# Block sums of w_out for the seven half-size products: added by DMA instead of by the vector engines

## The chip, the cores and the metric

The program runs on one core of one Trainium2 chip. The metric is the device time of one execution in microseconds (us). Five engines matter: TensorE (PE in the profile, its weight loads PEld), VectorE (DVE), ScalarE (ACT), GpSimd (POOL) and SyncE (SP), which in the kernel before issues every DMA. Each engine takes its instructions strictly in the order in which the program lists them; an instruction that waits holds up everything behind it on its engine.

## The reference, cut to what matters

A decoder layer: one input projection, two attention mixers, two branch projections, a gated merge, one output projection. The change touches only the last line, `merged @ w_out`, with `merged` of 512 x 1024 and `w_out` of 1024 x 1024, float32, and the residual `x` added.

```python
y_a = o_a * jax.nn.silu(z_a)
y_b = o_b * jax.nn.silu(z_b)
g_m = jax.nn.sigmoid(gate_m)
merged = g_m[..., :D_MODEL] * (y_a @ w_branch_a[l]) + g_m[..., D_MODEL:] * (y_b @ w_branch_b[l])
x = x + merged @ w_out[l]
```

## The kernel before, in words

**Arithmetic.** Every float32 product is made of three TensorE products of rounded halves: a tile is cast to a rounded high part (`wh`, `mh`, ...) and the rest is subtracted out as a low part (`wl`, `ml`, ...). So a weight block needs a load, a cast (ACT or POOL) and a subtraction (DVE or POOL) before TensorE can use it; the helper `mm3` (L399) then issues high x high, low x high, high x low.

**The output projection.** `merged` and `w_out` are cut in two by two blocks and multiplied by a scheme of seven half-size products instead of eight (Strassen's, in Winograd's form). A block of `w_out` is 512 x 512 and lies in four tiles of 128 x 512 (256 KB each), called b11, b12, b21, b22. The right factors of the products are: 1: b11; 7: b22 - b12; 5: t1 = b12 - b11; 6: t2 = b22 - t1; 2: b21; 3: b22; 4: b21 - t2. Four of the seven are sums, with four tiles each, so there are sixteen tile sums. A `Sum` object (L273 ff.) stands for one tile: `srcs` are its blocks in HBM, `keep` the number of a buffer `ws` in which t1 and then t2 stay, `prior` the sum that it continues, `home` says that its split halves go to the attention tiles' pool. All blocks are loaded by SP into rotating buffers `wq` (tag `ph`, six of them, shared with attention), then a `tensor_sub` on DVE or POOL makes the sum (L284, L286), then the split follows (L346, L348: cast; L350: low part).

**Order.** TensorE's work is listed by a generator per stream; the other engines' work is put in chains (`Chain`), each with planned costs, and a heap deals the chains' next steps to the engine that would end them first by those planned costs (`either` means DVE or POOL). What results is one fixed list per engine. Products 1 and 7 are made among the last branch projections (`EARLY`), the other five at the end in `output()`: first 5 and 6 interleaved, then 2, 3 and 4. SP's list holds block loads, the weight loads `wr` of gates and branches (`Stream.load`), the loads of the residual `xr`, and the stores.

Of the kernel before, what the change touches and what calls it, by code (L numbers as in the profile page):

```python
# [15 lines left out]
ALU = mybir.AluOpType  # L16
# [5 lines left out]
P = 128  # L22
# [20 lines left out]
LAT = 60  # L43
EARLY = {4:1,5:7}
PACE = 800
SHARE_A = 1.0
SHARE_F = 1.1
SHARE_C = 1.0
# [42 lines left out]
def hybrid_kernel(ctx: ExitStack, tc: tile.TileContext, x, x0, xT, wtok, wchan, gains, w1,  # L91
# [14 lines left out]
    def nm(s):  # L106
        uid[0] += 1
        return f"{s}{uid[0]}"
# [4 lines left out]
    now = [0.0]  # L113
    heap, seq = [], itertools.count()
    free = {"A": 1900.0, "D": 0.0, "P": 800.0, "Q": 400.0}
# [6 lines left out]
    held = {k: [] for k in RES}  # L122
    waiters = {k: [] for k in RES}
    owner, keep = {}, []
# [3 lines left out]
    def ca(n):  # L128
        return 93 + 0.834 * n

    def cap(n):
        return 51 + 0.834 * n

    def cd(n):
        return 65 + 1.045 * n

    def cg(n):
        return 180 + 2.08 * n
# [4 lines left out]
    def either(n):  # L143
        return {"d": cd(n), "P": cg(n)}
# [10 lines left out]
    class Chain:  # L155


        def __init__(c, t=None, held=False):
            c.t = now[0] if t is None else t
            c.q = deque()  # L160
            c.held = held
# [52 lines left out]
    def dma(dst, src, n, t=None):  # L214

        nc.sync.dma_start(out=dst, in_=src)
        free["Q"] = max(free["Q"], (now[0] if t is None else t) + 1000) + max(450, n * P / 360)
        return free["Q"] + 1000
# [6 lines left out]
    def alloc(tag, name, shape=(P, 512), dt=F32):  # L225
        pool, n = RES[tag]
        t = pool.tile(list(shape), dt, name=nm(name), tag=tag, bufs=n)
        keep.append(t)
        h = held[tag]
        if len(h) >= n:  # L230
            h.remove(min((z for z in h if z[0] is not None), key=lambda z: z[0]))
        owner[id(t)] = o = [None, tag]
        h.append(o)
        return t
# [4 lines left out]
    def release(t, when=None):  # L239
        o = owner[id(t)]  # L240
        o[0] = now[0] if when is None else when
        for c in waiters[o[1]]:
            c.t = max(c.t, o[0])
            c.push()
        waiters[o[1]].clear()
# [27 lines left out]
    class Sum:  # L273
# [2 lines left out]

        def __init__(z, srcs, keep=None, put=False, prior=None, home=False):
            z.srcs, z.keep, z.put, z.prior, z.home = srcs, keep, put, prior, home
            z.raw, z.t, z.c, z.left, z.next = [], 0.0, Chain(held=True), 1, None
            if prior:  # L280
                z.left += 1
                prior.next = z
            if len(srcs) == 2:
                z.c.do(either(512), lambda e: e.tensor_sub(z.dst(), z.raw[0], z.raw[1]), lambda: z.raw[1])  # L284
            elif keep is not None:
                z.c.do(either(512), lambda e: e.tensor_sub(z.dst(), z.raw[0], wsum[keep]))  # L286
            if put:
                z.c.call(lambda: release(z.raw[0], z.c.t))

        def dst(z):  # L290
            return wsum[z.keep] if z.put else z.raw[0]

        def fire(z, t):
            z.t = max(z.t, t)
            z.left -= 1
            if not z.left:
                z.c.start(max(now[0], z.t))

        def end(z):
            if not z.put:  # L300
                release(z.raw[0], z.c.t)
            if z.next:
                z.next.fire(z.c.t)

    wsum = []

    class Stream:
# [17 lines left out]
        def load_sums(w):  # L325
            ld = Chain()
            for z in w.tiles:
                if isinstance(z, Sum):
                    for src in z.srcs:
                        def f(z=z, src=src):  # L330
                            t = alloc("ph", "wq")
                            z.raw.append(t)
                            z.t = max(z.t, dma(t, src, 2048))
                        ld.do(None, f, None, "ph")
                    ld.call(lambda z=z: z.fire(z.t))

        def split_sum(w, i):
            z = w.tiles[i]
# [103 lines left out]
    def att(name, dt=F32R):  # L442
        return ap_.tile([P, 512], dt, name=nm(name), tag="a")
# [920 lines left out]
    def merged(c, j, m):  # L1364

        lo_, hi_ = slice(0, 256), slice(256, 512)
        a, b = att("mh"), att("ml")

        def sub(c, dst, x, y):
            c.do(either(256), lambda e: e.tensor_sub(dst, x, y))  # L1370

        def part(c, h, l, src):
            c.do({"A": ca(src.shape[-1])}, lambda e: e.copy(h, src))  # L1373
            c.do(either(src.shape[-1]), lambda e: e.tensor_sub(l, src, h.bitcast(F32)))
        if j < 4:
            q = att("ms", F32)
            sub(c, q[:, lo_], m[:, lo_], m[:, hi_])
            part(c, a[:, lo_], b[:, lo_], m[:, lo_])
            part(c, a[:, hi_], b[:, hi_], q[:, lo_])
            ms.append((m, q, c))  # L1380
            A11.append((a[:, lo_], b[:, lo_], c))
            S3.append((a[:, hi_], b[:, hi_], c))
            return
        i = j - 4
        n, q, prior = ms[i]
        assert not prior.q
        if i % 2 == 0:
            one.append((att("s1h"), att("s1l")))
        o = slice(i % 2 * 256, i % 2 * 256 + 256)
        u, v = (z[:, o] for z in one[-1])  # L1390
        x, y = att("sh"), att("sl")
        d, f = Chain(held=True), Chain(held=True)
        c.do(either(256), lambda e: e.tensor_add(q[:, hi_], n[:, hi_], m[:, hi_]))
        c.call(lambda: d.start(c.t))
        sub(c, n[:, lo_], q[:, hi_], n[:, lo_])
        sub(c, n[:, hi_], m[:, lo_], n[:, lo_])
        c.call(lambda: f.start(c.t))
        part(d, u, v, q[:, hi_])
        part(c, x, y, n)
        part(f, a, b, m)  # L1400
        A12.append((a[:, lo_], b[:, lo_], f))
        A22.append((a[:, hi_], b[:, hi_], f))
        S1.append((u, v, d))
        S2.append((x[:, lo_], y[:, lo_], c))
        S4.append((x[:, hi_], y[:, hi_], c))
# [36 lines left out]
                    if e == 4:  # L1442
                        f(t, (p, Chain(now[0] + 230)), o)

    def add(z, t, r, col, frees=False, o=slice(0, 512)):
        p, c = z
        key = 2 * r + t, col
        dst = xr[key]
        pend[key] = pend.get(key, 0) + 1
        c.do({"D": cd(o.stop - o.start)}, lambda e: e.scalar_tensor_tensor(  # L1450
            dst[:, o], p[:, o], 0.25, dst[:, o], op0=ALU.mult, op1=ALU.add), p if frees else None)
        c.call(lambda: pend.__setitem__(key, pend[key] - 1))

    def send(z, t, r, col, o=slice(0, 512)):
        key = 2 * r + t, col

        def f():
            assert pend[key] == (o.stop < 512 and not z[2:])
            dma(out[key[0] * P:(key[0] + 1) * P, col * 512 + o.start:col * 512 + o.stop], xr[key][:, o],
                4 * (o.stop - o.start))  # L1460
        z[1].call(f)
# [3 lines left out]
    def hold(z, name):  # L1465
        held_[name].append(z[0])
        z[1].mark(("read", id(z[0])))
# [8 lines left out]
    def out7():  # L1476
        def f(t, z, _):
            add(z, t, 1, 0)
            add(z, t, 1, 1)
            p = held_["1"][t]  # L1480
            z[1].do({"A": cap(512)}, lambda e: e.copy(z[0], p)).mark(("read", id(p)))
            hold(z, "7")
        yield from products((S3, "ss", f))
        i = tiles.index(right[5][0])
        for k in range(4):
            Chain(now[0] + PACE * k).call(lambda k=k: W.split_sum(i + k))

    early = {1: out1, 7: out7}

    def output():  # L1490
        def five(t, z, _):
            add(z, t, 1, 1)
            hold(z, "5")

        def six(t, z, _):
            add(z, t, 1, 1)
            send(z, t, 1, 1)
            add(z, t, 0, 1)
            hold(z, "6")
        yield from products((S1, "to", five), (S2, held_["7"], six))  # L1500
        for left, ps, r, col in ((A12, held_["1"], 0, 0), (S4, held_["5"], 0, 1), (A22, held_["6"], 1, 0)):
            def f(t, z, o):
                for q in (slice(0, 256), slice(256, 512)):
                    if o.start <= q.start < o.stop:
                        y = z if o.stop - o.start > 256 else (*z, 1)
                        add(z, t, r, col, q.stop == o.stop, q)
                        send(y, t, r, col, q)
            yield from products((left, ps + ps[1:] * (left is A22), f))
# [21 lines left out]
    now[0] = 3500.0  # L1530
    A, F, C, X = Run(attention(), SHARE_A), Run(gemms(), SHARE_F), Run(cmp(), SHARE_C), Run(x_rms(), 100.0)
    runs = [X, A, F, C]
    while any(r.live for r in runs):
# [9 lines left out]
        r = min(ok, key=lambda q: q.vt)  # L1543
# [80 lines left out]
```

## Time and profile before

| | |
|---|---|
| time, median of 3 runs | 468.33 us (467.44 to 468.35) |
| span of the profiled execution, first to last instruction | 466.7 us; it is the only time that the profile has of that execution, 1.6 us under the median of the timed runs |
| instructions | 7421 |
| TensorE clock granted, mean | 0.996 |
| DMA | 54.34 MB, mean 116 GB/s |

In the profile's rows a group is: line, engine, operation, `out<-in`, shape, count, busy time. In the timeline and the chain of waits the first column is the start and the second the length, both in us. A wait is shown in square brackets with the engine and line that ended it. In the table of stretches each engine has its busy time in us and its count of instructions, then come the granted clock, the mean busy share of the DMA engines and GB/s.

### The profile page before, as it was taken

The page shows a single profiled execution, that of the slowest core. Times are in us where ns is not written, and L with a number is a line of the kernel's source. Part 1 is how long each engine was busy: PE and PEld are TensorE (multiplying, and loading weights), DVE is VectorE, ACT ScalarE, POOL GpSimd, SP SyncE. Part 2 cuts the span into 40 slices and gives each one's busy share as a digit, 9 for nine tenths or more (in the row PEclk, how much of TensorE's full clock was granted, in tenths as well). Part 3 has the DMA queues.
Part 4 walks back from the last instruction along what each step waited for, and adds up shares of the span by engine and source line. Part 5 has one row for each costly group of instructions (what it writes and reads, how often), then busy time and mean ns, then how long its engine had stood idle before and what let it go on. Part 6 is the DMA issues. An engine that isn't in the chain of part 4 may idle for free.

```text
span 466.7 us, 7421 instructions
## 1 busy us (share of the span) xinstructions
PE 460.7 (99%) x2432; PEld 389.4 (83%) x2432; DVE 365.0 (78%) x852; ACT 264.1 (57%) x609; POOL 167.8 (36%) x215
## 2 busy tenths in 40 slices
PE   9989999999999999999999999999999999999997
PEld 8768887899788998888888888888888788887886
DVE  5767589788978868796877777687776887589994
ACT  7652547676677745656766653386765533263530
POOL 0115135644746323123554531455553140015110
PEclk9989999999999999999999999999999999999999
DMA  8752343364413622322223032301311588642162
GB/s 293 231 168 78 102 126 96 80 178 141 145 49 104 190 67 49 98 82 77 49 81 89 20 109 76 107 8 46 93 45 55 194 270 308 203 145 90 30 185 103
DMA packets 30486, 54.34 MB, mean 116 GB/s; under 512 B 3376, under 2 KB 5296, under 8 KB 30448
## 3 DMA queue, kind: packets, MB, share of 16 engines
q1 hardware_dynamic: 30448, 53.87, 38.1%
q8 instruction: 19, 0.31, 0.3%
q14 instruction: 19, 0.16, 0.1%
HBM read 51.11 MB, written 2.75 MB: 115 GB/s over the span
## 4 chain that ended last, share of the span: by engine, by line
PE 95%; DVE 2%; ACT 1%; issue 1%; DMA 1%; POOL 0%; DVEq 0%; ACTq 0%; POOLq 0%
PE pgc L399 31%; PE pgt L399 17%; PE pbr L399 9%; PE po L399 8%; PE O L1034 6%; PE pt L999 6%; PE pgf L609 5%; PE sps L952 3%; PE sps L953 3%; PE pq L896 1%; PE pw L457 1%; DVE wl L374 1%; PE hps L790 1%; PE hps L789 1%; PE scp L1125 1%
## 5 line engine op out<-in xcount | busy, mean ns | idle before, releaser
L399 PE MATMUL pgc<-hh,wh 128*128 128x512 f32 x208 | 84.2, 405 | 0.0
L399 PE MATMUL pgc<-hl,wh 128*128 128x512 f32 x208 | 82.0, 394 | 0.0
L399 PE MATMUL pgc<-hh,wl 128*128 128x512 f32 x208 | 81.7, 393 | 0.0
L374 DVE TENSOR_TENSOR wl<-wr,wh 128x512 fp32r<-128x512 f32 (+1 forms) x94 | 69.4, 754 | 7.8 <-ACT wh L370 4.1
L971 DVE CUSTOM_DVE_ANT_0 sb<-sps,T 128x512 f32<-128x512 f32 (+3 forms) x96 | 46.2, 485 | 22.1 <-PE sps L953 21.4
L399 PE MATMUL pgt<-wh,hh 128*128 128x512 f32 (+2 forms) x160 | 57.1, 357 | 0.2
L399 PE MATMUL pgt<-wl,hh 128*128 128x512 f32 (+2 forms) x160 | 56.2, 351 | 0.2 <-DVE wl L374 0.2
L986 ACT ACTIVATE P<-sb,sst 128x512 f32<-128x512 f32 (+3 forms) x88 | 51.0, 581 | 9.4 <-DVE sst L971 8.8
L399 PE MATMUL pgt<-wh,hl 128*128 128x512 f32 (+2 forms) x160 | 56.2, 351 | 0.0
L990 POOL TENSOR_SCALAR P<-P,sst,gate 128x512 f32<-128x512 f32 (+3 forms) x56 | 38.6, 694 | 43.1 <-DVE sst L989 41.3
L370 ACT CAST wh<-wr 128x512 fp32r<-128x512 f32 (+1 forms) x79 | 47.8, 618 | 7.0 <-DMA wr<-in_wchan 1.9
L1012 ACT CAST ph<-pt 128x512 fp32r<-128x512 f32 (+2 forms) x72 | 33.4, 479 | 29.0 <-PE pt L999 28.3
L399 PEld LDWEIGHTS pgc<-hl,wh 128*128 128x128 f32 x208 | 39.1, 188 | 9.0
L399 PEld LDWEIGHTS pgc<-hh,wh 128*128 128x128 f32 x208 | 39.2, 188 | 7.3 <-ACT s1h L1373 0.3
L399 PEld LDWEIGHTS pgc<-hh,wl 128*128 128x128 f32 x208 | 39.2, 188 | 7.2
L1014 DVE TENSOR_TENSOR pl<-pt,ph 128x512 fp32r<-128x512 f32 (+2 forms) x72 | 38.6, 550 | 5.3 <-ACT ph L1012 5.2
L999 PE MATMUL pt<-cst,P 128*128 128x128 f32 x232 | 40.7, 272 | 0.0
L990 POOL TENSOR_SCALAR P<-P,sst 128x512 f32<-128x512 f32 (+3 forms) x32 | 20.1, 632 | 56.8 <-DVE sst L989 49.8
L399 PEld LDWEIGHTS pgt<-wl,hh 128*128 128x128 f32 x160 | 30.1, 188 | 4.9 <-DVE wl L374 0.7
L399 PEld LDWEIGHTS pgt<-wh,hh 128*128 128x128 f32 x160 | 30.1, 188 | 4.5 <-PE pgt L399 0.3
L999 PEld LDWEIGHTS pt<-cst,P 128*128 128x128 f32 x232 | 29.2, 140 | 4.8 <-POOL P L990 0.7
L399 PEld LDWEIGHTS pgt<-wh,hl 128*128 128x128 f32 x160 | 30.1, 188 | 3.5
(242 smaller groups left out, 1063.6 us busy)
## 6 DMA issues: line engine op xcount, KB each, us to landing
wr<-in_wchan SPq DMA_DIRECT2D x52, 256.0 KB, 2.9
wr<-in_wtok SPq DMA_DIRECT2D x36, 256.0 KB, 3.9
wq<-in_wout SPq DMA_DIRECT2D x36, 256.0 KB, 2.9
T<-rtab SPq DMA_DIRECT2D x16, 256.0 KB, 3.9
wr<-in_w SPq DMA_DIRECT2D x16, 256.0 KB, 3.5
wr<-in_wbr SPq DMA_DIRECT2D x16, 256.0 KB, 3.9
xr<-in_x SPq DMA_DIRECT2D x8, 256.0 KB, 5.7
x<-in_xT SPq DMA_DIRECT2D x7, 256.0 KB, 5.0
```

What stands on the lines that cost most here:

```text
L370: e.copy(hi, raw)
L374: c.do(either(n), lambda e, hi=hi, lo=lo, raw=raw: e.tensor_sub(lo, raw, hi.bitcast(F32))).mark((w, 1, i))
L399: nc.tensor.matmul(dst, sts[i][a], mvs[i][b], start=(start and i == a == b == 0), stop=(stop and i == n - 1 and b == 1), skip_group_check= ...
L609: nc.tensor.matmul(ps[t][:, :n], (hl if a else hh)[:, k, t * P:(t + 1) * P], ws[k][b], start=(k == a == b == 0), stop=(k == KT - 1 and b = ...
L952: nc.tensor.matmul(sps[:, :n], qs[:, b * P:(b + 1) * P], ks[:, :n], start=True, stop=False)
L971: e.tensor_tensor_reduce(z["sb"][:, :L], sps[:, :L], T[:, S - L:], scale=-1.0, scalar=3e38, op0=ALU.add, op1=ALU.min, accum_out=st[:, 0, b ...
L986: e.activation(pv(), z["sb"][:, :L], AF.Exp, bias=st[:, 0, b:b + 1], scale=-1.0, accum_out=st[:, 1, b:b + 1])
L990: c.do({"P": 315 + 0.834 * L}, lambda e: e.tensor_scalar(pv(), pv(), st[:, 2, b:b + 1], g, op0=ALU.mult, op1=ALU.mult))
L999: nc.tensor.transpose(pt[:, (b - kb) * P:(b - kb + 1) * P], u.p0 if u.p0 is not None and b == 0 else u.pb[:, POFF[b] + kb * P:POFF[b] + (k ...
L1012: e.copy(z["w"][0], pt[:, :w])
L1014: ch.do({"D": cd(w)}, lambda e: e.tensor_sub(z["w"][1], pt[:, :w], z["w"][0].bitcast(F32)), pt)
L1034: nc.tensor.matmul(O[0][:, S - n:], v.bitcast(F32) if kb == 3 else v, w, start=(u.first and kb == 0 and i == 0), stop=(u.last and kb == 3 ...
```

## The change

The sixteen subtractions leave DVE and POOL. The first block of a sum is loaded by SP as before; every further block is fetched by a DMA that POOL issues with `accum_op=add`, so the DMA itself adds the block in HBM to the tile in SBUF. Such a DMA can only add, so the signs are moved: the blocks are now sums (7: b22 + b12; t1 = b12 + b11; t2 = b22 + t1; 4: b21 + t2), two of the sums of `merged` change sign (`tensor_add` and `tensor_sub` trade places, same size), and three of the additions into `xr` take the factor -0.25. t1 is loaded straight into its `ws` tile; t2 and 4 add onto the same tile, after its split for the earlier product has been read. Twenty blocks are loaded by SP (36 before), sixteen by POOL. The planner counts 1000 ns of POOL for such a DMA (`ACC`), some 3.2 us more until it lands (`landing`), and keeps the first loads 2000 ns apart (`SPREAD`).

```diff
+ACC = 1000
+SPREAD = 2000
@@ class Sum
-            if len(srcs) == 2:
-                z.c.do(either(512), lambda e: e.tensor_sub(z.dst(), z.raw[0], z.raw[1]), lambda: z.raw[1])
-            elif keep is not None:
-                z.c.do(either(512), lambda e: e.tensor_sub(z.dst(), z.raw[0], wsum[keep]))
-            if put:
-                z.c.call(lambda: release(z.raw[0], z.c.t))
+            for src in srcs[not prior:]:
+                z.c.do({"p": ACC}, lambda e, src=src: e.dma_start(out=z.dst(), in_=src, accum_op=ALU.add))
+                z.c.call(z.landing)
+
+        def landing(z):
+            free["Q"] = max(free["Q"], z.c.t + 1000) + 2048 * P / 360
+            z.c.t = free["Q"] + 1500
 
         def dst(z):
-            return wsum[z.keep] if z.put else z.raw[0]
+            return z.raw[0] if z.keep is None else wsum[z.keep]
...
@@ load_sums
-                if isinstance(z, Sum):
-                    for src in z.srcs:
-                        def f(z=z, src=src):
-                            t = alloc("ph", "wq")
-                            z.raw.append(t)
-                            z.t = max(z.t, dma(t, src, 2048))
-                        ld.do(None, f, None, "ph")
-                    ld.call(lambda z=z: z.fire(z.t))
+                if isinstance(z, Sum) and not z.prior:
+                    def f(z=z):
+                        if z.keep is None:
+                            z.raw.append(alloc("ph", "wq"))
+                        z.fire(dma(z.dst(), z.srcs[0], 2048))
+                    ld.do(None, f, None, "ph" if z.keep is None else None)
+                    ld.call(lambda: setattr(ld, "t", ld.t + SPREAD))
@@ merged
-        c.do(either(256), lambda e: e.tensor_add(q[:, hi_], n[:, hi_], m[:, hi_]))
+        sub(c, q[:, hi_], n[:, hi_], m[:, hi_])
...
-        sub(c, n[:, hi_], m[:, lo_], n[:, lo_])
+        c.do(either(256), lambda e: e.tensor_add(n[:, hi_], m[:, lo_], n[:, lo_]))
@@ add, out7, six
-    def add(z, t, r, col, frees=False, o=slice(0, 512)):
+    def add(z, t, r, col, frees=False, o=slice(0, 512), sign=0.25):
...
-            add(z, t, 1, 1)
+            add(z, t, 1, 1, sign=-0.25)
...
-            add(z, t, 0, 1)
+            add(z, t, 0, 1, sign=-0.25)
```

TensorE's list is the same 2255 rows in the same order. The lists of the other engines differ from the start of the block loads on: POOL loses ten vector instructions (one block sum; six others go to DVE, three casts to ACT) and gets the sixteen DMAs; DVE loses fifteen block sums.

POOL, first part, where the sums for products 7 and 5 are made. Before (`wr` are weights of gates and branches, `wq` blocks of `w_out`, `ml`/`mh` halves of `merged`):

```order
L348 TENSOR_SCALAR wh_4737<-wq_4659 128x512
L374 TENSOR_TENSOR wl_4775<-wr_4706,wh_4774 128x512
L1374 TENSOR_TENSOR ml_4777<-gm_3223,mh_4776 128x256
L372 TENSOR_SCALAR wh_4852<-wr_4797 128x512
L374 TENSOR_TENSOR wl_4871<-wr_4809,wh_4870 128x512
L348 TENSOR_SCALAR wh_5109<-wq_4792 128x512
```

and of the change (L285 is the accumulating DMA):

```order
L285 DMA wq_4724<-in_wout 128x512
L285 DMA wq_4756<-in_wout 128x512
L285 DMA wq_4783<-in_wout 128x512
L370 TENSOR_SCALAR wh_4845<-wr_4786 128x512
L285 DMA wq_4801<-in_wout 128x512
L285 DMA ws_4645<-in_wout 128x512
L285 DMA ws_4646<-in_wout 128x512
L285 DMA ws_4647<-in_wout 128x512
L285 DMA ws_4648<-in_wout 128x512
L346 TENSOR_SCALAR wh_5089<-wq_4801 128x512
```

Eight DMAs now stand here; the cast of a gate's weights (`wh_4845`) is behind three of them, the cast for product 7 (`wh_5089`) behind all eight.

POOL, second part, from the split of t1 to the end. Before:

```order
L350 TENSOR_TENSOR wl_5175<-ws_4645,wh_5174 128x512
L286 TENSOR_TENSOR ws_4646<-wq_5054,ws_4646 128x512
L1370 TENSOR_TENSOR gm_3223<-ms_4778,gm_3223 128x256
L372 TENSOR_SCALAR wh_5267<-wr_5168 128x512
L1374 TENSOR_TENSOR ml_5209<-gm_3778,mh_5208 128x512
L348 TENSOR_SCALAR wh_5348<-ws_4647 128x512
L350 TENSOR_TENSOR wl_5357<-ws_4648,wh_5356 128x512
L348 TENSOR_SCALAR wh_5414<-wq_5229 128x512
L350 TENSOR_TENSOR wl_5458<-wq_5243,wh_5457 128x512
```

and of the change:

```order
L348 TENSOR_TENSOR wl_5156<-ws_4645,wh_5155 128x512
L285 DMA ws_4645<-in_wout 128x512
L285 DMA ws_4646<-in_wout 128x512
L285 DMA ws_4647<-in_wout 128x512
L285 DMA ws_4648<-in_wout 128x512
L285 DMA ws_4645<-in_wout 128x512
L346 TENSOR_SCALAR wh_5328<-ws_4648 128x512
L285 DMA ws_4646<-in_wout 128x512
L285 DMA ws_4647<-in_wout 128x512
L285 DMA ws_4648<-in_wout 128x512
L348 TENSOR_TENSOR wl_5429<-wq_5108,wh_5428 128x512
```

Eight more DMAs follow the split of t1's first tile; the last row, the low part of a tile of product 3 (b22), is behind all of them.

DVE near the end, in the last products. Before:

```order
L1450 SCALAR_TENSOR_TENSOR xr_4831<-po_5111,xr_4831 128x512
L286 TENSOR_TENSOR wq_5429<-wq_5429,ws_4645 128x512
L1450 SCALAR_TENSOR_TENSOR xr_4832<-po_5144,xr_4832 128x512
L1450 SCALAR_TENSOR_TENSOR xr_4829<-po_5111,xr_4829 128x512
L1450 SCALAR_TENSOR_TENSOR xr_4830<-po_5144,xr_4830 128x512
L286 TENSOR_TENSOR wq_5449<-wq_5449,ws_4646 128x512
L350 TENSOR_TENSOR wl_5472<-wq_5258,wh_5471 128x512
```

and of the change:

```order
L1448 SCALAR_TENSOR_TENSOR xr_4825<-po_5091,xr_4825 128x512
L1448 SCALAR_TENSOR_TENSOR xr_4826<-po_5122,xr_4826 128x512
L1448 SCALAR_TENSOR_TENSOR xr_4823<-po_5091,xr_4823 128x512
L1448 SCALAR_TENSOR_TENSOR xr_4824<-po_5122,xr_4824 128x512
L348 TENSOR_TENSOR wl_5443<-wq_5127,wh_5442 128x512
```

The subtractions for product 4 are gone from between the additions into the output.

More of the change, by code (lines that the diff above doesn't have):

```diff
@@ L278, in __init__ @@
             z.srcs, z.keep, z.put, z.prior, z.home = srcs, keep, put, prior, home
-            z.raw, z.t, z.c, z.left, z.next = [], 0.0, Chain(held=True), 1, None
+            z.raw, z.t, z.c, z.next = [], 0.0, Chain(held=True), None
             if prior:
-                z.left += 1
                 prior.next = z
-            if len(srcs) == 2:
-                z.c.do(either(512), lambda e: e.tensor_sub(z.dst(), z.raw[0], z.raw[1]), lambda: z.raw[1])
-            elif keep is not None:
-                z.c.do(either(512), lambda e: e.tensor_sub(z.dst(), z.raw[0], wsum[keep]))
-            if put:
-                z.c.call(lambda: release(z.raw[0], z.c.t))
+            for src in srcs[not prior:]:
[4 more added lines that the diff above has]
+            z.c.t = free["Q"] + 1500
         def dst(z):
-            return wsum[z.keep] if z.put else z.raw[0]
+            return z.raw[0] if z.keep is None else wsum[z.keep]
         def fire(z, t):
[L294 to L297, printed above, removed]
+            z.c.start(max(now[0], t))
         def end(z):
-            if not z.put:
+            if z.keep is None:
                 release(z.raw[0], z.c.t)
@@ L327, in load_sums @@
             for z in w.tiles:
-                if isinstance(z, Sum):
-                    for src in z.srcs:
-                        def f(z=z, src=src):
-                            t = alloc("ph", "wq")
-                            z.raw.append(t)
-                            z.t = max(z.t, dma(t, src, 2048))
-                        ld.do(None, f, None, "ph")
-                    ld.call(lambda z=z: z.fire(z.t))
+                if isinstance(z, Sum) and not z.prior:
+                    def f(z=z):
+                        if z.keep is None:
+                            z.raw.append(alloc("ph", "wq"))
+                        z.fire(dma(z.dst(), z.srcs[0], 2048))
+                    ld.do(None, f, None, "ph" if z.keep is None else None)
+                    ld.call(lambda: setattr(ld, "t", ld.t + SPREAD))
         def split_sum(w, i):
@@ L1450, in add @@
         c.do({"D": cd(o.stop - o.start)}, lambda e: e.scalar_tensor_tensor(
-            dst[:, o], p[:, o], 0.25, dst[:, o], op0=ALU.mult, op1=ALU.add), p if frees else None)
+            dst[:, o], p[:, o], sign, dst[:, o], op0=ALU.mult, op1=ALU.add), p if frees else None)
         c.call(lambda: pend.__setitem__(key, pend[key] - 1))
@@ L1495, in six @@
         def six(t, z, _):
-            add(z, t, 1, 1)
+            add(z, t, 1, 1, sign=-0.25)
             send(z, t, 1, 1)
-            add(z, t, 0, 1)
+            add(z, t, 0, 1, sign=-0.25)
             hold(z, "6")
```

## Prediction

> **What bounds the kernel now.** I read the page's busy shares first, then the chain of waits over the end of the program, then the table of stretches for the same time.
>
> ```profile
> span 466.7 us, 7421 instructions
> PE 460.7 (99%) x2432; PEld 389.4 (83%) x2432; DVE 365.0 (78%) x852; ACT 264.1 (57%) x609; POOL 167.8 (36%) x215
> ```
>
> TensorE is idle for 466.7 - 460.7 = 6.0 us of the whole span. The question is how much of that lies where the change works. The chain of waits, from the first block load on:
>
> ```profile
> 364.73 0.81 DVE yl L1077
> 365.54 0.04 issue
> 365.58 0.50 PE pbr L399
> 366.08 5.51 PE pgc L399 x24
> ...
> 396.62 5.46 PE po L399 x24
> ...
> 427.08 5.70 PE pgc L399 x24
> 432.79 2.79 PE pbr L399 x12
> 435.58 27.80 PE po L399 x132
> 463.38 0.02 issue
> 463.40 0.42 DVE xr L1450
> ```
>
> From 365.58 to 463.38 the chain is TensorE alone: nothing that DVE or POOL does in these 98 us is waited for. The stretches say the same and show who else is close:
>
> ```profile
> 380.00:396.00 16.00, 16.00 (x70) 12.97 (x69) 11.99 (x19) 5.86 (x12) 3.23 (x4) 1.00 0.88 296
> 396.00:418.00 22.00, 22.00 (x97) 17.93 (x96) 15.11 (x27) 8.38 (x17) 0.00 (x0) 1.00 0.60 196
> 418.00:435.00 17.00, 17.00 (x75) 13.60 (x74) 16.91 (x27) 7.35 (x16) 7.28 (x6) 1.00 0.20 63
> 446.00:463.00 17.00, 17.00 (x86) 14.27 (x85) 13.71 (x28) 3.11 (x5) 0.00 (x0) 1.00 0.46 147
> ```
>
> TensorE is busy in every microsecond. DVE is nearly full from 418 to 435 (16.91 of 17.00) but keeps ahead of its deadlines; POOL is at rest for most of the time.
>
> **What the change removes.** The sixteen sums stand in the rows of the block tiles:
>
> ```profile
> L284 DVE TENSOR_TENSOR wq<-wq,wq x4: 676/680/692, 369.8 to 382.2; 128x512 f32<-128x512 f32 x4
> L284 DVE TENSOR_TENSOR ws<-wq,wq x4: 676/693/693, 390.6 to 403.8; 128x512 f32<-128x512 f32 x4
> L286 DVE TENSOR_TENSOR wq<-wq,ws x4: 679/682/685, 447.3 to 454.7; 128x512 f32<-128x512 f32 x4
> L286 DVE TENSOR_TENSOR ws<-wq,ws x3: 676/680/1781, 420.5 to 425.2; 128x512 f32<-128x512 f32 x3
> L286 POOL TENSOR_TENSOR ws<-wq,ws x1: 1680/1680/1680, 420.0 to 420.0; 128x512 f32<-128x512 f32 x1
> ```
>
> On DVE that is 14 x 0.68 + 1.78 = 11.3 us, on POOL 1.7 us. DVE takes six instructions over from POOL, at most 6 x 0.68 = 4.1 us, so it is freed of some 7 us; ACT takes three casts of 0.62. All of it lay beside TensorE's 98 us, so on the path the removal is worth **nothing**: TensorE's list is unchanged, row for row. Could TensorE itself run faster beside a quieter DVE? Between 366.08 and 463.38 it issues 420 matmuls' worth of 512 columns (nine pieces of 24, seven of 12, and 120 in the piece of 132, whose last 24 are half size). The best piece takes 5.46 us for 24, 0.2275 us each; 420 of these are 95.6 us, and the trace has 97.3. So 1.7 us is the most that smoother running could give. I take 0: the traffic by DMA, which stays (36 blocks either way), is as likely behind it as DVE. The tail (last product, addition of 0.42 us, store) is unchanged.
>
> Flipped signs cost nothing: `tensor_add` and `tensor_sub` of the same size trade places, and a factor of -0.25 is an operand.
>
> **What the change adds: sixteen DMAs in POOL's list, and what is queued behind them.** No DMA issued by POOL and none that adds is in this trace. What matters is T, from POOL's start on one to its landing, and whether the next can start before that. Nearest rows:
>
> ```profile
> wq<-in_wout SPq DMA_DIRECT2D x36, 256.0 KB, 2.9
> L216 SPq DMA_DIRECT2D wq<-in_wout x36: 327/328/578, 359.3 to 451.0; - x36
> q1 hardware_dynamic: 30448, 53.87, 38.1%
> ```
>
> A plain load of the same block lands 2.9 us after its issue, of which SP spends 0.33. The lower bound of T is that, 2.9. The upper bound is two such loads one after the other, since the DMA must read the old tile as well: 5.8. In between: a packet takes 0.381 x 16 x 466.7 / 30448 = 0.093 us of one of 16 engines; a block has 128 rows, eight for each engine, 0.75 us; a second read adds 0.75. For POOL's issue I take the planner's 1.0 us in place of SP's 0.33. So T = 2.9 + 0.75 + 0.67 = **4.3 us**, an estimate between these ends.
>
> Whether they overlap I bound from both sides. If they do, POOL is held 16 x 1.0 = 16 us in 85 us in which it has little to do, and TensorE waits for nothing. If each has to wait for the one before to land, POOL works them off at one per T, and three places decide. Their rows, TensorE's need beside POOL's work:
>
> ```profile
> 374.62 1.86 POOL L374 TENSOR_TENSOR wl<-wr,wh 128x512 fp32r<-128x512 f32 x1 [8.01 <-ACT wh L370]
> 380.40 0.62 POOL L372 TENSOR_SCALAR wh<-wr 128x512 fp32r<-128x512 f32 x1
> 394.03 0.89 POOL L348 TENSOR_SCALAR wh<-wq 128x512 fp32r<-128x512 f32 x1 [9.95 <-PE pgc L399]
> 418.11 1.30 POOL L350 TENSOR_TENSOR wl<-ws,wh 128x512 fp32r<-128x512 f32 x1 [23.19 <-DMA wr<-in_wbr]
> 444.35 1.30 POOL L350 TENSOR_TENSOR wl<-wq,wh 128x512 fp32r<-128x512 f32 x1 [5.35 <-ACT wh L346]
> ```
> ```profile
> 385.33 0.39 PE L399 MATMUL pgc<-hh,wh 128*128 128x512 f32 x1
> 412.36 0.39 PE L399 MATMUL po<-wh,mh 128*128 128x512 f32 x1
> 452.45 0.39 PE L399 MATMUL po<-wl,sh 128*128 128x512 f32 x1
> ```
>
> (1) The cast of gate weights (0.62) is behind three DMAs and is needed at 385.33. POOL is at rest before 374.62, and I put the first DMA there at the latest: 374.6 + 2T + 1.0 + 0.62 <= 385.33, so T up to 4.5 is free, and more if the first starts earlier. (2) The cast for product 7 (0.89) is behind eight and is needed at 412.36: 374.6 + 7T + 1.0 + 0.89, T up to 5.1. (3) The second eight can start when t1's first tile is split, at 418.11 + 1.30 = 419.41, since the second block is added onto that tile. Behind them stands the low part of b22's first tile (1.30), which the product at 452.45 reads; before it was ready at 445.65. Now: 419.41 + 7T + 1.0 + 1.30 = 421.71 + 7T, so **T up to 4.39 us is free, and every 0.1 us beyond it costs 0.7 us**. At T = 4.3 it is ready at 451.8, 0.6 us early.
>
> So with my T the sum is 0 overlapped and 0 one at a time, the second with little to spare. The cover of product 4's sums is thinner too: the last lands at 419.41 + 8T = 453.8, with 0.62 + 0.68 of splitting needed before TensorE reads it near 458.
>
> The Trainium skill speaks for one at a time. Its page "DMA: Bandwidth & Descriptors", section "SWDGE vs HWDGE vs iDMA", says that accumulating DMAs are issued from GpSimd alone, whose descriptors go to rings in a carved-out part of SBUF; its section "Terms" gives 16 bytes for a descriptor. The kernel asks for 512 bytes of that part (L1613), by an estimate from that page 32 descriptors for each DMA engine; eight rows with two reads each and, by the section "The descriptor swizzle", a closing one are 17, so a second DMA would not fit beside the first. By this rule the sum goes by place (3), without it by the overlapped case. The section "Anatomy of one DMA" fits a plain transfer from GpSimd as 2.0 us plus bytes / 436e3, 2.6 us here, by which nothing would be late even one at a time; no run here shows either yet.
>
> **The rivals.**
>
> *One at a time, and T over 4.39 (slower).* For it: ends of T lie at 2.9 and 5.8, and my value is 0.1 us from the limit. Against it: the 0.67 us for POOL's issue and the full second read may both be too much. Price by place (3): T = 4.6 costs 1.5 us, T = 5.0 costs 421.71 + 35.0 - 452.45 = 4.3 us (472.6), T = 5.8 costs 9.9 us, and the first two places then begin to add to it. TensorE would wait at product 3, for POOL.
>
> *Queues in disorder (slower by 1 to 2 us, some 469.7).* SP's list is put in a new order, with weights and blocks mixed, and three casts moved to ACT. A gate's weights that land late by one load (2.9 us) would be seen by TensorE as 1 to 2 us where the DMA share is already 0.88 (380 to 396). Against it: SP issues sixteen loads fewer.
>
> *Smoother running (faster).* TensorE gets back half or more of the 1.7 us, 467.2. For it: DVE is full from 418 to 435 and gets relief just there. Against it: TensorE is listed as busy throughout.
>
> *The sums are not really off the engines.* The lists show that they are; what could come back is only time, as above.
>
> **How the numbers follow.** The profiled execution has a span of 466.7, which is 1.6 us under the median of the runs, 468.33. The likeliest case, no wait on TensorE, adds 0 to either: 468.3, chance 0.52 (its own range 467.4 to 469.2). Slower by T 0.30, slower by the queues 0.08, faster 0.10. Within 0.2% (0.9 us) is about what a measurement of this kernel can tell from no change. The range reaches up to T = 5.0 or a little more (473.0) and down to the smoother case (467.2); T beyond that and larger gains are the rest.
>
> **What would show it.** Right: TensorE without idle time from 366 to the end, DVE's busy time some 7 us lower, POOL's DMAs landing within 4.4 us each. One at a time or not is seen in POOL's rows: starts of neighbouring DMAs a whole T apart, or 1 us. Wrong by T: weight loads of product 3 waiting for POOL's low part near 452, with the eight DMAs before it more than 4.39 us apart. Wrong by queues: TensorE's waits at gates and branches between 380 and 435, ended by ACT casts. Wrong by smoothness: the piece of 132 products shorter than 27.8 us.

## The result, and the profile after

| kernel | median, us | range, us | ratio to the kernel before, 95% interval |
|---|---|---|---|
| before (20 executions) | 468.34 | 466.82 to 471.84 | |
| changed (20 executions) | 470.59 | 468.45 to 473.94 | 1.0051 (1.0032 to 1.0071) |

The change makes the kernel slower by 0.5%, 2.25 us between the medians. The profiled execution took 469.91 us with a span of 468.1 us. The page of the changed kernel, its totals, its two kinds of queue (packets, MB, share of sixteen engines) and the DMA issues that are new or changed (count, size, median us from issue to landing; line numbers are lower by two than before, so L397 is the matmul helper; the row of `wq` by POOL is from the DMA view, since the page stops short of it):

```profile
PE 461.7 (99%) x2432; PEld 389.4 (83%) x2432; DVE 354.5 (76%) x843; ACT 264.6 (57%) x612; POOL 169.6 (36%) x221
q1 hardware_dynamic: 28144, 49.68, 33.8%
q0 software_dynamic: 2304, 4.20, 5.9%
ws<-in_wout POOLq DMA_DIRECT2D x12, 256.0 KB, 4.0
xr<-in_x SPq DMA_DIRECT2D x8, 256.0 KB, 6.9
wq<-in_wout POOLq DMA_DIRECT2D x4, 256.0 KB, 7.1
```

DVE is freed of 365.0 - 354.5 = 10.5 us, some 3 more than forecast: subtractions that stay on it became shorter too (from 355 us on, 19 of `wl<-wr,wh` take 797 ns each in the mean before, 22 take 695 ns after; no run says why). Twelve of the sixteen DMAs, those into `ws`, land after 4.0 us in the median, near the 4.3 of the prediction; the four into `wq`, which come first, land after 7.1. POOL's timeline for the first eight accumulating DMAs (L285) and the two casts behind them shows what follows from that (start, length, in brackets the idle time before it):

```profile
371.65 1.08 POOL L285 DMA_DIRECT2D wq<-in_wout  x1 [6.32 <-DMA wq<-in_wout]
376.18 0.90 POOL L285 DMA_DIRECT2D wq<-in_wout  x1 [3.45 <-issue]
383.83 0.88 POOL L285 DMA_DIRECT2D wq<-in_wout  x1 [6.76 <-issue]
384.41 0.95 POOL L370 TENSOR_SCALAR wh<-wr 128x512 fp32r<-128x512 f32 x1
390.87 0.92 POOL L285 DMA_DIRECT2D wq<-in_wout  x1 [5.51 <-DVE gm L1265]
398.63 0.88 POOL L285 DMA_DIRECT2D ws<-in_wout  x1 [6.83 <-issue]
402.86 0.89 POOL L285 DMA_DIRECT2D ws<-in_wout  x1 [3.35 <-issue]
407.17 0.87 POOL L285 DMA_DIRECT2D ws<-in_wout  x1 [3.42 <-issue]
411.72 0.88 POOL L285 DMA_DIRECT2D ws<-in_wout  x1 [3.68 <-issue]
412.31 0.95 POOL L346 TENSOR_SCALAR wh<-wq 128x512 fp32r<-128x512 f32 x1
```

The DMAs go one at a time: each row of some 0.9 us is the issue, and the idle time ahead of it is POOL held until the DMA before has landed. (Whatever the brackets name, in this trace each issue within the two groups of eight starts some 0.3 us after the landing of the one before.) The distances are 4.5, then 7.7, 7.0 and 7.8, then 4.2, 4.3 and 4.6 us. The mean over the seven is (411.72 - 371.65) / 7 = 5.7 us, not 4.3. The cast for product 7 (L346) stands behind all eight, and the waits of TensorE's weight loads in that stretch name it, and then a low part on POOL (us in total, times, longest):

```profile
PEld po L397 <- POOL wh L346: 0.5, 1, 0.5
PEld po L397 <- DVE wl L348: 0.4, 1, 0.4
PEld po L397 <- POOL wl L348: 0.2, 1, 0.2
```

None of these three stands in the profile of before. The second is the same lateness once more: DVE makes that low part from the late cast.

### The profile page after: what moved, and what is told of

Read it like the earlier page. It is cut to its first block, busy times and chain, and to the rows that moved or that the text cites. A ratio compares the mean times of both kernels' runs of the same rounds, so it can differ in the third digit from the quotient of the medians.

```text
span 468.1 us, 7413 instructions
## 1 busy us (share of the span) xinstructions
PE 461.7 (99%) x2432; PEld 389.4 (83%) x2432; DVE 354.5 (76%) x843; ACT 264.6 (57%) x612; POOL 169.6 (36%) x221
## 4 chain that ended last, share of the span: by engine, by line
PE 75%; DMA 9%; DVE 6%; issue 5%; ACT 3%; POOL 1%; SPq 1%; DVEq 0%; ACTq 0%; POOLq 0%
PE pgc L397 26%; PE pgt L397 12%; PE pbr L397 7%; PE po L397 7%; PE O L1032 6%; PE pt L997 5%; PE sps L950 3%; PE sps L951 3%; DMA wr<-in_wtok 2%; DVE wl L372 2%; DMA wq<-in_wout 2%; DMA wr<-in_w 2%; DMA ws<-in_wout 1%; PE pgf L607 1%; DMA xr<-in_x 1%
## 5 line engine op out<-in xcount | busy, mean ns | idle before, releaser
L397 PE MATMUL pgc<-hh,wh 128*128 128x512 f32 x208 | 84.1, 404 | 0.0
L397 PE MATMUL pgc<-hl,wh 128*128 128x512 f32 x208 | 82.0, 394 | 0.0
L397 PE MATMUL pgc<-hh,wl 128*128 128x512 f32 x208 | 81.8, 393 | 0.0
L397 PE MATMUL pgt<-wh,hh 128*128 128x512 f32 (+2 forms) x160 | 57.1, 357 | 0.2
L397 PE MATMUL pgt<-wl,hh 128*128 128x512 f32 (+2 forms) x160 | 56.2, 351 | 0.3 <-DVE wl L372 0.3
L397 PE MATMUL pgt<-wh,hl 128*128 128x512 f32 (+2 forms) x160 | 56.2, 351 | 0.0
L397 PEld LDWEIGHTS pgc<-hl,wh 128*128 128x128 f32 x208 | 39.1, 188 | 8.9
L397 PEld LDWEIGHTS pgc<-hh,wl 128*128 128x128 f32 x208 | 39.2, 188 | 7.3
L397 PEld LDWEIGHTS pgc<-hh,wh 128*128 128x128 f32 x208 | 39.2, 188 | 7.1
L997 PE MATMUL pt<-cst,P 128*128 128x128 f32 x232 | 40.7, 272 | 0.0
L397 PEld LDWEIGHTS pgt<-wl,hh 128*128 128x128 f32 x160 | 30.1, 188 | 4.9 <-DVE wl L372 0.7
L397 PEld LDWEIGHTS pgt<-wh,hh 128*128 128x128 f32 x160 | 30.1, 188 | 4.5 <-PE pgt L397 0.3
L397 PEld LDWEIGHTS pgt<-wh,hl 128*128 128x128 f32 x160 | 30.1, 188 | 3.5
```

The costliest lines, as they stand in the source:

```text
L397: nc.tensor.matmul(dst, sts[i][a], mvs[i][b], start=(start and i == a == b == 0), stop=(stop and i == n - 1 and b == 1), skip_group_check= ...
L997: nc.tensor.transpose(pt[:, (b - kb) * P:(b - kb + 1) * P], u.p0 if u.p0 is not None and b == 0 else u.pb[:, POFF[b] + kb * P:POFF[b] + (k ...
```

## The experiments

The theories on trial. **A**: the ring of descriptors (512 bytes) holds one accumulating DMA; POOL is held for each landing, so its casts come late. **B**: the extra traffic of the adding slows the loads. **C**: the new order of loads and casts is at fault. A2, A3, A2p and A3p are finer questions inside A.

Single profiles scatter ahead of the changed stretch, where the lists hardly differ: the 430th matmul from the last starts between 364.33 us (both_off) and 368.86 us (ring_576). So I also give for each profile how long TensorE takes from that matmul to its last one, cut in three at the 240th and the 132nd from the end. The table has the excess over the profile of before (43.89, 25.15 and 27.67 us), worked out from the matmuls' starts in the traces. The first part holds the prediction's place (1), the cast of gate weights; the second place (2), the cast for product 7; the third place (3), the low part for product 3, and product 4.

| kernel | median, us | ratio, 95% interval | excess: place 1 | place 2 | place 3 and on | sum |
|---|---|---|---|---|---|---|
| changed | 470.59 | 1.0051 (1.0032 to 1.0071) | 0.00 | 0.50 | 0.09 | 0.59 |
| after_again | 471.10 | 1.0048 (1.0015 to 1.0081) | 0.01 | 0.63 | 1.98 | 2.6 |
| after_third | 471.46 | 1.0077 (1.0051 to 1.0102) | 1.07 | 1.00 | 0.82 | 2.9 |
| ring_576 | 468.65 | 1.0007 (0.9982 to 1.0031) | 0.24 | -0.11 | 0.00 | 0.1 |
| plain_blocks | 469.04 | 1.0004 (0.9978 to 1.0030) | 0.03 | -0.11 | 0.00 | -0.1 |
| half_blocks | 468.25 | 0.9992 (0.9962 to 1.0022) | 0.57 | -0.11 | 0.00 | 0.5 |
| casts_off | 468.25 | 0.9999 (0.9971 to 1.0027) | 0.06 | -0.11 | 0.32 | 0.3 |
| planner_4400 | 470.79 | 1.0047 (1.0020 to 1.0073) | 0.01 | 0.72 | 0.32 | 1.1 |
| cast7_off | 471.92 | 1.0090 (1.0061 to 1.0118) | 0.00 | -0.11 | 2.15 | 2.0 |
| low3_off | 470.04 | 1.0039 (1.0013 to 1.0065) | 0.33 | 0.68 | 0.39 | 1.4 |
| both_off | 468.19 | 1.0016 (0.9991 to 1.0040) | 1.32 | -0.11 | 0.57 | 1.8 |

The first three rows are one kernel. Its three profiles lose 0.6, 2.6 and 2.9 us in these stretches, 2.0 in the mean, at different places each time; that is about the size of the 2.25 us between the medians. Each excess is that of one execution, against one execution of the kernel before. Each ratio is to executions of the kernel before on the same chip, and the rows come from several chips, so the ratios can be compared across rows and the medians only within a chip.

**The changed kernel again.** No edit.

> The changed kernel once more, as the base of the runs beside it. Theory A (the descriptor ring of 512 bytes holds one accumulating DMA, so POOL is held until each lands, 4.3 us when the loads are quiet and about 7 us between 376 and 398, and TensorE waits for POOL's casts): 1.005 times the kernel before (1.003 to 1.007), starts of neighbouring DMAs on POOL 4.3 to 7.7 us apart, TensorE's weight loads waiting for POOL between 410 and 456 by 0.5 us or more in sum. Theory B (the second read of SBUF and the slower packets take bandwidth from the loads): the same time, but waits that DMAs end. Theory C (the new order of the loads and casts): the same time, with waits at gates and branches.

Measured: 1.0048. This execution lost most at place 3, the low part for product 3 behind sixteen DMAs. Its second eight DMAs start at 420.00 and 452.23, 32.23 / 7 = 4.60 us apart in the mean, over the 4.39 that the prediction called free. Two rows of its waits, first the weight loads and then the matmuls:

```profile
PEld po L397 <- POOL wl L348: 2.1, 1, 2.1
PE po L397 <- POOL wl L348: 1.7, 1, 1.7
```

**A larger ring.**

```diff
-dynamic_dma_scratch_size=512
+dynamic_dma_scratch_size=576
```

> The ring of POOL's descriptors is 576 bytes in place of 512 (an estimate: room for two accumulating DMAs instead of one); every engine's list of instructions is that of the changed kernel. Theory A: DMAs start in pairs on POOL, two starts about 1 us apart, the casts behind them come 4 us earlier or more, no wait of TensorE for POOL is left, and the time falls back to 0.998 to 1.002 of the kernel before. Theory B: two transfers at a time make the loads slower still, 1.005 or more. Theory C: 1.005, as the changed kernel.

Measured: 1.0007, no wait for POOL in its profile, an excess of 0.1 us. POOL's timeline, the first two DMAs (the "x2" row is two issues in a row) and the cast for product 7 behind the eighth:

```profile
374.32 1.99 POOL L285 DMA_DIRECT2D wq<-in_wout  x2 [6.85 <-DMA wq<-in_wout]
...
402.89 0.95 POOL L346 TENSOR_SCALAR wh<-wq 128x512 fp32r<-128x512 f32 x1
```

Sixty-four bytes let two DMAs be under way, and from the first DMA's start to the cast behind the eighth it takes 28.6 us, against 40.7 before the edit. All engines' lists, the bytes moved and the loads' order are those of the changed kernel, and on the same chip the changed kernel's median is 471.10 against 468.65 here. B has 1.005 or more here and C 1.005: A is shown.

**Copies in place of additions.** Left out is the adding, so that each sum is its last block.

```diff
-e.dma_start(out=z.dst(), in_=src, accum_op=ALU.add)
+e.dma_start(out=z.dst(), in_=src)
```

> Left out is the adding: POOL's sixteen DMAs are plain copies, so each sum is its last block; the lists are otherwise those of the changed kernel. Theory A: a plain copy takes half the descriptors, so two or three fit in the ring, and starts are about 1 us apart for the first ones; no wait of TensorE for POOL, 0.998 to 1.002 of the kernel before. Theory B: the second read is gone, also 0.998 to 1.002, but landings shorter in the stretch from 380 to 400 even where they are alone. Theory C: 1.005.

Measured: 1.0004. Its first two copies are issued back to back, 1.32 us for both, and no wait for POOL is left. By itself this fits A and B; beside ring_576, where all the adding stays, it is A.

**The planner's price.**

```diff
-ACC = 1000
+ACC = 4400
```

> The planner counts 4.4 us of POOL for each of the sixteen DMAs in place of 1.0, with the ring as it is; it takes the cast of gate weights, one cast of product 4's sums and the low part of b22's first tile off POOL, and leaves the cast for product 7 there, behind eight DMAs. TensorE's list and that of the loads are those of the changed kernel. Theory A: the wait at product 7 stays, 0.3 to 0.8 us, the others go: 1.001 to 1.005 of the kernel before. Theories B and C: 1.005, and starts of DMAs as far apart as in the changed kernel in every theory.

Measured: 1.0047. The wait for the cast of product 7 stayed (0.72 us in the table), place 3 is clear of POOL. The ratio is at the upper end of A's range and, with its interval, in no theory's way: it tells little that the others don't. Its profile loses 1.1 us, about half of what the ratio stands for.

**Nothing left behind the DMAs.** The ring stays at 512; casts of sums are tied to ACT, their low parts to DVE, and the planner's price is 4.4 us, which takes the gate weights' cast off too.

```diff
-ACC = 1000
+ACC = 4400
...
-            c.do({"A": ca(512), "P": 78 + 512}, f)
-            c.do(either(512), lambda e: e.tensor_sub(lo, z.dst(), hi.bitcast(F32)))
+            c.do({"A": ca(512)}, f)
+            c.do({"d": cd(512)}, lambda e: e.tensor_sub(lo, z.dst(), hi.bitcast(F32)))
```

> The ring stays at 512 bytes and the sixteen accumulating DMAs stay; the casts and low parts of the sums are tied to ACT and DVE, and the planner counts 4.4 us for each DMA, so that nothing stands behind the DMAs in POOL's list. Lists of TensorE and of the loads are those of the changed kernel. Theory A (POOL is held, and its casts come late): neighbouring DMAs start as far apart as in the changed kernel (4.1 to 7.7 us), no wait of TensorE for POOL, 0.999 to 1.002 of the kernel before. Rival A2 (the sums themselves land too late, whoever casts them): TensorE waits for DVE's low parts or ACT's casts of product 7 near 412 or of product 4 near 455, 1.003 to 1.005.

Measured: 0.9999. The DMAs are as slow as ever: POOL's rows start at 370.93, 375.23, 382.45, 389.65 and 397.30. They cost nothing, because nothing that TensorE reads stands behind them. A2 is left with a small part: the last DMA of this profile starts at 451.74, and TensorE waits for a low part of product 4 on DVE (0.32 us in the table). The same wait is in planner_4400, low3_off and both_off, and in none of the three variants in which several DMAs are under way at once (ring_576, plain_blocks, half_blocks).

**Halves of 64 partitions.**

```diff
-                z.c.do({"p": ACC}, lambda e, src=src: e.dma_start(out=z.dst(), in_=src, accum_op=ALU.add))
+                for o in (slice(0, 64), slice(64, 128)):
+                    z.c.do({"p": ACC}, lambda e, src=src, o=o: e.dma_start(out=z.dst()[o], in_=src[o], accum_op=ALU.add))
```

> Ring of 512 bytes; each of the sixteen DMAs is split in two of 64 partitions, 32 DMAs with the same bytes in all. By theory A (the ring is full by the count of descriptors: an estimate of 9 for a half against 17 for a block) three halves are under way at once: starts about 1 us apart in threes, POOL is held 32 x 0.9 = 29 us for issuing but less for waiting, TensorE's waits for POOL are smaller than 0.5 us in sum, 0.999 to 1.003. Rival (one accumulating DMA at a time, whatever its size): starts a whole landing apart for each half, 32 x 3 us or more, so POOL's casts are later than in the changed kernel and the time is 1.005 or more.

Measured: 0.9992, no wait for POOL. The first row of L285 and the cast for product 7:

```profile
371.24 2.73 POOL L286 DMA_DIRECT2D wq<-in_wout  x3 [6.11 <-PE pgc L398]
403.86 0.92 POOL L347 TENSOR_SCALAR wh<-wq 128x512 fp32r<-128x512 f32 x1
```

Three start at once where one whole block did, with the ring unchanged. Twice as many DMAs end sooner: the cast starts 32.6 us after the first issue, against 40.7. So what fills the ring is neither the count of DMAs nor that of bytes (three halves are 384 KB, one block is 256). (The line numbers of this kernel are higher by one.) Its 0.57 us at the first place are waits for gate weights split on DVE and ACT, after a load that landed late.

**The DMA by itself.** Left out is the whole computation. POOL issues four DMAs of a kind, waits for all, and goes on to the next kind; last, SP issues forty loads of 256 KB beside four accumulating blocks.

> Left out is the whole computation; the kernel only moves blocks of w_out, with a ring of 512 bytes. POOL issues four at a time: accumulating 128x512, plain 128x512, accumulating 64x512, accumulating 128x256, and again accumulating 128x512 while SP issues forty loads without a pause. Theory A: accumulating blocks alone start 4.0 to 4.4 us apart, plain ones and halves of 64 partitions about 1 us apart for the first two or three, halves of 256 columns one at a time and 3 to 4.2 us apart, and blocks beside the forty loads 6 to 8 us apart. Rival A3 (the 7 us between 376 and 398 come from a first block that had not landed yet, not from the load on the DMA engines): 4.0 to 4.4 us apart beside the loads too.

POOL's timeline, of each kind the first DMA rows (L101 accumulates, L115 copies): whole blocks, copies, halves of 64 partitions, halves of 256 columns, and whole blocks beside the loads:

```profile
2.58 1.02 POOL L101 DMA_DIRECT2D a<-in_wout  x1
6.71 0.90 POOL L101 DMA_DIRECT2D a<-in_wout  x1 [3.10 <-issue]
11.02 0.87 POOL L101 DMA_DIRECT2D a<-in_wout  x1 [3.42 <-issue]
15.25 0.88 POOL L101 DMA_DIRECT2D a<-in_wout  x1 [3.36 <-issue]
...
19.91 1.70 POOL L115 DMA_DIRECT2D a<-in_wout  x3
...
27.04 2.62 POOL L101 DMA_DIRECT2D a<-in_wout  x3
...
34.17 0.88 POOL L101 DMA_DIRECT2D a<-in_wout  x1
37.59 0.88 POOL L101 DMA_DIRECT2D a<-in_wout  x1 [2.54 <-issue]
...
48.41 0.89 POOL L101 DMA_DIRECT2D a<-in_wout  x1
53.70 0.87 POOL L101 DMA_DIRECT2D a<-in_wout  x1 [4.40 <-issue]
61.48 0.89 POOL L101 DMA_DIRECT2D a<-in_wout  x1 [6.91 <-issue]
68.53 0.87 POOL L101 DMA_DIRECT2D a<-in_wout  x1 [6.17 <-issue]
```

Alone, a block takes (15.25 - 2.58) / 3 = 4.22 us; beside the loads (68.53 - 48.41) / 3 = 6.71 (5.3, 7.8 and 7.0; the first is under the 6 that was expected). So A3 is out: with nothing but loads running beside it, a block is nearly as slow as the 7.0 to 7.8 between 376 and 398. Halves of 256 columns, with half the bytes on as many partitions, still go one at a time, 3.4 us each; halves of 64 partitions and copies start in threes. The packets of POOL's queue say what the two groups have in common; four halves of 256 columns, then four copies (packets, MB, share):

```profile
q0 software_dynamic: 576, 0.52, 28.2%
q0 software_dynamic: 320, 1.05, 45.8%
```

Whole blocks have 576 too, halves of 64 partitions 320. What has 144 packets a DMA goes one at a time, what has 80 goes in threes, whatever the bytes.

**The same with a ring of 1024 bytes.**

> The same with a ring of 1024 bytes, computation left out as before. Theory A: three accumulating blocks start about 1 us apart and the fourth waits for the first to land; plain blocks, 64-partition halves and 256-column halves never wait for more than the fourth's issue. If landings share bandwidth, four blocks take more than 4.4 us from the first start to the first landing but less than 4 x 4.3 us in all. Rival (the number under way isn't set by the ring): spacings as with 512.

```profile
2.59 2.83 POOL L101 DMA_DIRECT2D a<-in_wout  x3
7.22 0.89 POOL L101 DMA_DIRECT2D a<-in_wout  x1 [1.80 <-issue]
```

Three accumulating blocks start at once and the fourth 4.63 us after the first, as A expects. All four have landed 9.4 us after the first start, against 16.7 with 512 bytes. Four copies and four 64-partition halves start without a wait in this run. The 256-column halves again start in threes.

**Two instructions, one by one.** The last four runs move the cast of place 2 and the low part of place 3 off POOL, alone and together, at 512 bytes and the planner's 1.0 us.

```diff
-            c.do({"A": ca(512), "P": 78 + 512}, f)
+            c.do({"A": ca(512)} if z in right[7] else {"A": ca(512), "P": 78 + 512}, f)
```

> One instruction of the changed kernel is moved: the cast of product 7's last sum goes from POOL, where it stands behind eight DMAs, to ACT; the low part for product 3 stays on POOL behind sixteen. If that low part is the dearer place (theory A3p: the second eight take 4.4 to 4.7 us each, so it is 0.1 to 2 us late, and whatever product 7 no longer waits is waited for here instead): 1.003 to 1.006 of the kernel before, no wait at product 7, a wait of 0.5 to 3 us for POOL's low part near 452. If product 7 is the dearer place (theory A2p): 0.999 to 1.002.

```diff
-            c.do(either(512), lambda e: e.tensor_sub(lo, z.dst(), hi.bitcast(F32)))
+            c.do({"d": cd(512)} if z in right[3] else either(512), lambda e: e.tensor_sub(lo, z.dst(), hi.bitcast(F32)))
```

> The other one alone: the low parts for product 3 are tied to DVE, the cast for product 7 stays on POOL behind eight DMAs. Theory A3p: only the wait at product 7 is left, 0.3 to 1.0 us, 1.001 to 1.003 of the kernel before. Theory A2p: 1.004 to 1.006.

Both edits:

> Both moves together, ring of 512 bytes and the planner's 1.0 us as in the changed kernel. Both theories: 0.999 to 1.002 of the kernel before, no wait of TensorE for POOL. If the time stays above 1.003, a third place is in play (the cast of gate weights behind three DMAs, or the cast of product 4's last sum behind thirteen).

No edit:

> The changed kernel once more on the same chip as the base of the three: 1.003 to 1.007 of the kernel before; the second eight DMAs start 4.4 to 4.7 us apart in the mean, and TensorE's waits for POOL near 412 and 453 are 0.6 to 3 us in sum.

Measured: cast7_off 1.0090, low3_off 1.0039, both_off 1.0016, the changed kernel beside them 1.0077. Clearing place 2 alone gains nothing, as A3p has it: TensorE comes sooner to product 3 and waits there instead (1.9 us of matmuls for POOL's low part in its profile). The 1.0090 lies above A3p's 1.006, and I have no reason for its being higher than the changed kernel's own 1.0077; their intervals overlap. Clearing place 3 alone gives some of it back, and its 1.0039 lies between A3p (1.001 to 1.003) and A2p (1.004 to 1.006); both together give back nearly all. But the expectation of no wait for POOL failed in both_off, and for after_third I named only the places near 412 and 453 and a ratio of at most 1.007. Weight loads in the profile of both_off, then in that of after_third:

```profile
PEld pgc L397 <- POOL wh L370: 1.0, 1, 1.0
```
```profile
PEld po L397 <- POOL wh L346: 1.0, 1, 1.0
PEld po L397 <- POOL wl L348: 1.0, 1, 1.0
...
PEld pgc L397 <- POOL wh L370: 0.8, 1, 0.8
```

That is place 1, the cast of gate weights behind three DMAs. In both_off its third DMA starts 382.44 - 369.75 = 12.7 us after the first, 6.3 us each. In after_third one execution shows all three places late. The 1.8 us that the profile of both_off loses are more than its ratio stands for; how often place 1 is late, single profiles can't tell.

No run beats the kernel before: with no wait for POOL left, TensorE takes the time that it took before.

## Why the prediction was wrong

**Right.** TensorE alone sets the end, and the subtractions were worth nothing: in the variants without waits for POOL (ring_576, half_blocks, casts_off) DVE is as relieved as in the changed kernel and the time is that of before, so smoother running, the faster rival, gave nothing that the times can show. In ring_576 and half_blocks the last 132 products take the 27.67 us of before, the stretch ahead of them 0.11 us less. One at a time is right, by the ring: the Trainium skill's page "DMA: Bandwidth & Descriptors", sections "Terms" and "The descriptor swizzle", gave the estimate of 17 descriptors for a block against 32, and the runs agree (one block at 512 bytes, two at 576, three at 1024; halves of 64 partitions, 9 by the same estimate, in threes at 512). No view counts descriptors; the packets of dma_alone, 144 and 80 a DMA, fall into the same two groups. The Trainium skill's fit in the same page's section "Anatomy of one DMA" gives 2.6 us for a plain block, which is near what copies take in quiet stretches here (the last eight of plain_blocks land after 2.8 to 3.1 us), but not what accumulating blocks take (3.9 to 4.1 us alone). The three places were the right ones, and each was seen late. The quiet T was near: 4.3 predicted, 4.22 alone from start to start. That is in part luck, since the 4.22 are a landing of 3.9 to 4.1 us and some 0.3 us until the next issue, a term that the sum did not have, and no run measured the sum's three terms apart.

**Wrong.** The step that failed is the size of T, in the sentence "T = 2.9 + 0.75 + 0.67 = 4.3 us, an estimate between these ends", with 5.8 as the upper end. It took one T for the whole program, from a median landing over 359 to 451 us, and its upper end is no bound. Between 376 and 398 T was 7.0 to 7.8. The trace of before had this in the stretch itself: DMA issues from 366 to 400 us, and the row of the stretch from 376 on (engines' busy time, clock, DMA share, GB/s):

```profile
wq<-in_wout SPq DMA_DIRECT2D x12, 256.0 KB, 3.1
xr<-in_x SPq DMA_DIRECT2D x8, 256.0 KB, 5.7
wr<-in_wchan SPq DMA_DIRECT2D x7, 256.0 KB, 5.1
376.00:400.00 24.00, 24.00 (x105) 19.51 (x105) 17.75 (x29) 8.70 (x17) 4.35 (x5) 1.00 0.85 281
```

Plain loads of 256 KB into `wr` and `xr` took 5.1 and 5.7 us there, at a DMA share of 0.85, though those of the blocks themselves only 3.1. With the prediction's own 0.75 and 0.67 on top, 5.1 and 5.7 would have given a T of 6.5 to 7.1. After the change the share is 0.96:

```profile
376.00:400.00 24.00, 24.00 (x106) 19.54 (x105) 15.04 (x29) 8.20 (x17) 4.23 (x5) 1.00 0.96 314
```

Places 1 and 2 were to be free up to a T of 4.5 and 5.1. Place 1 had (383.83 - 371.65) / 2 = 6.1 and was still in time in this profile, because its first DMA started 3 us earlier than the 374.6 that the prediction took as the latest. At place 2 the mean of the first eight was 5.7: the cast for product 7 ended at 412.31 + 0.95 = 413.26 us, needed at 412.36 in the profile of before and 0.7 us later here, since TensorE came to this stretch that much later (367.10 against 366.38 for the 430th matmul from the last).

**Place 3 had the right formula and no margin.** Free up to 4.39 against a T of 4.3 is 0.09 us for each of seven DMAs. The first and the last of the second eight in the changed kernel, and the low part behind them:

```profile
420.37 0.91 POOL L285 DMA_DIRECT2D ws<-in_wout  x1 [0.41 <-POOL wl L348]
...
451.40 0.87 POOL L285 DMA_DIRECT2D ws<-in_wout  x1 [3.20 <-DVE xr L1448]
451.97 1.62 POOL L348 TENSOR_TENSOR wl<-wq,wh 128x512 fp32r<-128x512 f32 x1
```

The second eight measured 4.43 (changed), 4.60 and 4.55 us (its two other profiles), because the last of them meet loads again: in the changed kernel the DMA share is 0.62 from 436 to 456, and one distance there is 447.32 - 441.70 = 5.6 us. At 4.60 the rival's price is 7 x 0.21 = 1.5 us; the profile with 4.60 lost 1.98 in that part. So the rival "one at a time, and T over 4.39" happened, and "no wait on TensorE" as the likeliest case was the wrong choice. But the rival had the loss begin at place 3. By its formula the 4.43 of the changed kernel's profile costs 421.71 + 7 x 4.43 - 452.45 = 0.3 us, and place 2, at which it had nothing, lost 0.50 there. That the measured 470.59 lies inside the stated range is therefore not a sign that the places were priced right.

**The three places do not add up simply.** I wrote that the first two would begin to add at T = 5.8. They were late first, and what TensorE loses at place 2 it need not lose again at place 3: clearing place 2 alone brought no gain.

**Queues in disorder** had a small part at most. In ring_576 and half_blocks a load of gate weights landed late, and TensorE waited for the split (0.24 and 0.57 us at place 1 in the table); ring_576, with the order of the changed kernel, is still within 0.3% of before. The waits for gate weights split on DVE in the profiles of cast7_off, low3_off, both_off and after_third are another thing: DVE works there from POOL's late cast at place 1. Whether 0.2 to 0.6 us of disorder are left on average stays open.

## What to carry to other kernels

Price a DMA by the slowest landings of its neighbours in the stretch in which it will run, not by its kind's median over the program. If an engine issues DMAs through a ring, as POOL does here, ask how many DMAs the ring holds at once, because here a full ring held that engine for some 3 to 7 us at a time, and with it every instruction listed behind. Then either make room (64 bytes were enough here), cut the DMA into pieces of fewer partitions, or put nothing urgent behind it.

## What the runs showed of the hardware

That a DMA's duration in POOL's rows, 0.9 us, leaves out the time that POOL is held: it shows as idle time put down to "issue", or to whatever ended near it. That halving an accumulating DMA's columns leaves it as hard on the ring (144 packets) and only 0.8 us shorter (3.4 against 4.22 us), while halving its partitions (80 packets) lets three run at once. And that one accumulating block slows from 4.22 to 6.71 us beside a full queue of loads.
